# The order of a Winograd tail, the order of its loads, the queue of its stores, and the additional matmuls, in a hybrid decoder block

## The chip, the cores and the metric

The kernel runs on one core of a Trainium2 chip. The metric is the device time of one execution in microseconds; lower is better. Time before: 2496.36 us, the median of 3 runs (2493.04 to 2498.78).

## What is computed

One layer of a decoder trunk on 512 tokens of width 2048, all in float32:

```python
h = rmsnorm(x, g_mix)
z = h @ w_in                       # 2048 x 10248
cb, cc, cv, q, k, v, f_logit, gate_c, gate_a = split(z)
conv_y = cb * causal_dwconv(cc * cv, conv_w)            # three taps
conv_branch = conv_y @ w_conv_out
attn = forgetting_attention(q, k, v, log_sigmoid(f_logit + b_f))   # 8 heads of 128, causal
attn_branch = attn @ w_attn_out
merged = sigmoid(gate_c + b_c) * conv_branch + sigmoid(gate_a + b_a) * attn_branch
x = x + merged @ w_mix_out
h = rmsnorm(x, g_mlp)
u = square(relu(h @ w_ff1))        # 2048 x 8192
x = x + u @ w_ff2
out = rmsnorm(x, g_final)
```

## The kernel before

**Products.** Each float32 operand is split in two parts of TensorE's rounded float32 type: ScalarE writes the high part `hi` (line 100), VectorE the low part `lo` as the difference (line 101). A product is three matmuls: high times high, high times low, low times high.

**Groups.** The products with `w_in` and `w_ff1` are done by Strassen's method in Winograd's form, seven products of half size in place of eight. The weights of two column blocks are four tiles `x00`, `x10`, `x01`, `x11` (1 MB each, [128, 8, 256]; first index: even or odd row blocks of 128, second: column block). The seven products have the names A11, A12, S1, S2, S3, S4, A22, after the sum of quarters of the activations that each needs; these sums, split in high and low parts, are made once for a whole stage. A `Group` (class at line 168) is done in two pieces: `head` makes A11 and A12, `tail` the other five. One product is a `run` (line 189): split the weights' tile into a pair of buffers `th`, `tl` (two of each), then 48 matmuls of 256 columns (`mm_cols`, line 126; `mm_rows`, line 145, for v). All matmuls with the high part come first, 32 of them, then the 16 with the low part. The accumulators a, b, c, d are banks of PSUM; `snap` (line 197) copies one to a tile `o` on ScalarE (five such tiles), `plus` (line 207) adds one to such a tile on VectorE, and `put` stores the result or passes it on.

In the tail of before, the order is S4, S2, S3, S1, A22. S4 uses the loaded `x11` as it is; the four others need differences of tiles, made in place on VectorE (line 104; 2048 elements for each partition):

```python
self.run(c, "S4", X[1, 1], True)
sub(X[0, 0], X[0, 1], X[0, 0])
sub(X[0, 1], X[1, 1], X[0, 1])
sub(X[1, 1], X[1, 1], X[0, 0])
self.run(a, "S2", X[1, 1], False)
```

There are four slots for weights' tiles; `load` takes the slot that came free first, `done` gives one back.

**The stages, in order.** Norm and transposes of x; heads of one v group and four k/q groups (about 24 to 85 us of the profile); the sums of activations; the five tails (85 to 231 us); one more v group of 260 columns; then six groups for the convolution's inputs, with the eight attention heads before the first four of them (275 to 480 us) and the eight jobs of the convolution (line 566) after them; eight groups for the gates (to 880 us); the two branch products and the mix product (to 1235 us); the sixteen groups of the first feed-forward product (to 1858 us; the first two have their heads ahead of both tails); the second feed-forward product and the last norm. Intermediate results go through device memory: `v_d`, `kq_d`, `z_d`, `g_d`, `y_d`, `a_d` and, for the squared feed-forward sums, `s_d`.

**Queues.** Loads of weights are issued from SP's queue (line 183), and so are the stores to `v_d`, `kq_d`, `z_d`, `g_d`, `y_d`, `a_d`. GpSimd's queue has the stores to `s_d` and `x1_d`, the loads of the sums and of x's blocks, and GpSimd's own few operations, among them a memset of two columns of `u` in each convolution job (line 571). Each queue, and each engine, takes its instructions in order. What order that is, a planner decides: it walks the program and gives out instructions by its own estimate of when they are ready, so that an engine's order is not always that of the text. Waits are put in from the data that instructions read and write.

**Additional matmuls.** `apart` (line 581) returns a function that `mm_cols` calls ahead of the matmuls of each q in the high part of S4. In before it issues two matmuls with 256 columns, at q = 2 and q = 5, into a bank `spare` that nobody reads. They are in one of the convolution's groups, three of the gates' and four of the feed-forward's.

Of the kernel before, what the change touches and what calls it, by code (L numbers as in the profile page):

```python
# [15 lines left out]
P = 128  # L16
# [4 lines left out]
HS = S // 2  # L21
# [15 lines left out]
QSCALE = float(P) ** -0.5  # L37
# [8 lines left out]
def tile_hybrid_block(ctx: ExitStack, tc, x, g_mix, w_in, b_f, b_gate, conv_w, w_conv_out,  # L46
# [79 lines left out]
    def mm_cols(ps, Sx, hi, lo, first, extra=None):  # L126


        ps = ps[0].rearrange("p (j s) -> p j s", j=2)
        nq = hi.shape[1]  # L130
        for part in range(2):
            for q in range(nq):
                Sh, Sl = Sx(q)
                if extra and part == 0:
                    extra(q, Sh, hi[:, q, :])
                for j in range(2):
                    o, js = ps[:, j, :], slice(j * P, (j + 1) * P)
                    if part == 0:
                        nc.tensor.matmul(o, hi[:, q, js], Sh, start=first and q == 0 and j == 0, stop=False,  # L139
                                         skip_group_check=True)  # L140
                        nc.tensor.matmul(o, hi[:, q, js], Sl, start=False, stop=False, skip_group_check=True)  # L141
                    else:
                        nc.tensor.matmul(o, lo[:, q, js], Sh, start=False, stop=q == nq - 1, skip_group_check=True)  # L143
# [24 lines left out]
    class Group:  # L168
# [67 lines left out]
            self.put(0, 0, s1)  # L236

        def tail(self):
            if self.at:
                X = self.X  # L240
            else:
                X = {(i, 0): self.load(i, 0) for i in range(2)}
            X[0, 1], X[1, 1] = self.load(0, 1), self.load(1, 1)
            a = self.a
            c = self.acc("c")
            self.run(c, "S4", X[1, 1], True)
            sub(X[0, 0], X[0, 1], X[0, 0])
            sub(X[0, 1], X[1, 1], X[0, 1])
            sub(X[1, 1], X[1, 1], X[0, 0])
            self.run(a, "S2", X[1, 1], False)  # L250
            sub(X[1, 0], X[1, 0], X[1, 1])
            self.done(1, 1)
            s2 = self.snap(a)
            while later:
                later.pop(0)()
            d = self.acc("d")
            self.run(d, "S3", X[0, 1], True)
            self.done(0, 1)
            d1 = self.snap(d, self.scale)
            self.run(a, "S1", X[0, 0], False)  # L260
            self.done(0, 0)
            s4 = self.snap(a, self.scale)
            add(d1, d1, s4)
            self.put(1, 1, d1)
            self.plus(s4, c, self.scale)
            self.put(0, 1, s4)
            self.run(d, "A22", X[1, 0], False)
            self.done(1, 0)
            self.plus(s2, d)
            self.put(1, 0, s2)  # L270
# [162 lines left out]
    def store_v(c0, w):  # L433
        def put(i, j, v):
            c = c0 + j * w
            n = min(w, AW - c)
            nc.sync.dma_start(out=v_d[2 * i:2 * i + 2, :, c:c + n].rearrange("t p c -> p t c"), in_=v[:, :, :n])
            if n < w:
                add(fl[:, 2 * i:2 * i + 2, :], v[:, :, n:], bf.unsqueeze(1).to_broadcast([P, 2, NH]))
        return put  # L440

    def store_kq(hp):
        def put(i, j, v):
            nc.sync.dma_start(out=kq_d[j, 2 * hp:2 * hp + 2, :, i * HS:(i + 1) * HS].rearrange("b p c -> p b c"), in_=v)
        return put

    cV = COL_AV + AW // 2
# [1 line left out]
    gV0 = Group(w_in, COL_AV, COL_AV + VW, VW, Q1.moving, mm_rows, ((4,), (3,), (6,), (7,)), store_v(0, VW))  # L449

    def kq(hp, banks):
        return Group(w_in, COL_K + hp * HS, COL_Q + hp * HS, HS, Q1.moving, mm_cols, banks, store_kq(hp), QSCALE)

    def steady(n):
        return ((2 + n % 2,), (3 - n % 2,), (0,), (1,))
# [73 lines left out]
    def attend(h):  # L529
        kT, qT = at("kT"), at("qT")  # L530
        nc.sync.dma_start(out=kT, in_=kq_d[0, h])
        nc.sync.dma_start(out=qT, in_=kq_d[1, h])
        vv = at("vv", [P, NT, P])
        nc.sync.dma_start(out=vv, in_=v_d[:, :, h * P:(h + 1) * P].rearrange("t p c -> p t c"))
        o = bank(4, "o")
        for qi in range(NT):
            n = (qi + 1) * P
            qs = slice(qi * P, n)
            sc = bank(5 + 2 * (qi % 2), "sc")
            nc.tensor.matmul(sc[:, :n], qT[:, qs], kT[:, :n], start=True, stop=False)  # L540
# [12 lines left out]
            nc.vector.tensor_scalar(out=p[:, :n], in0=p[:, :n], scalar1=rs, scalar2=None, op0=ALU.mult)  # L553
            tp = bank(6, "tp")
            for ki in range(qi + 1):
                nc.tensor.transpose(tp[:, ki * P:(ki + 1) * P], p[:, ki * P:(ki + 1) * P], ident)
            pt = at("pt")
            nc.vector.tensor_copy(pt[:, :n], tp[:, :n])
            for ki in range(qi + 1):
                nc.tensor.matmul(o[:, qs], vv[:, ki, :], pt[:, ki * P:(ki + 1) * P], start=(ki == 0), stop=(ki == qi))  # L560
        ov = at("ov")
        nc.scalar.activation(out=ov, in_=o, func=AF.Copy)
        nc.sync.dma_start(out=a_d[h], in_=ov)


    def conv_job(f):
        cv, cc, cb = at("cv"), at("cc"), at("cb")
        for k, t in enumerate((cb, cc, cv)):
            nc.sync.dma_start(out=t, in_=z_d[k, f])
        u = at("u", [P, S + 2])  # L570
        nc.gpsimd.memset(u[:, 0:2], 0.0)
        nc.vector.tensor_tensor(out=u[:, 2:], in0=cv, in1=cc, op=ALU.mult)
        w = [cwT[:, i * CT + f:i * CT + f + 1] for i in range(3)]
        y = at("y")
        nc.vector.tensor_scalar(out=y, in0=u[:, 0:S], scalar1=w[0], scalar2=None, op0=ALU.mult)
        for i in (1, 2):
            nc.vector.scalar_tensor_tensor(out=y, in0=u[:, i:S + i], scalar=w[i], in1=y, op0=ALU.mult, op1=ALU.add)
        nc.vector.tensor_tensor(out=y, in0=cb, in1=y, op=ALU.mult)
        nc.sync.dma_start(out=y_d[f], in_=y)

    def apart(i):


        spare = bank(i, "spare")

        def extra(q, Sh, h):
            if q in (2, 5):
                nc.tensor.matmul(spare[:, :HS], Sh[:, :P], Sh if q == 2 else h, start=True, stop=True)
        return {"S4": extra}

    n = 0
    for g in (4, 2, 0, 5, 3, 1):
        def put_z(i, j, v, g=g):
            f = 4 * (g % 2) + 2 * j
            nc.sync.dma_start(out=z_d[g // 2, f:f + 2, :, i * HS:(i + 1) * HS].rearrange("b p c -> p b c"), in_=v)
# [10 lines left out]
    for f in range(0, KT, 2):  # L606
        def put_g(i, j, v, f=f):
            for b in range(2):
                k = j * KT + f + b
                nc.scalar.activation(out=v[:, b, :], in_=v[:, b, :], func=AF.Sigmoid, bias=bgT[:, k:k + 1])  # L610
            nc.sync.dma_start(out=g_d[j, f:f + 2, :, i * HS:(i + 1) * HS].rearrange("b p c -> p b c"), in_=v)
# [259 lines left out]

    def ff1(g, banks):
        return Group(w_ff1, g * S, g * S + HS, HS, Q2.moving, mm_cols, banks, put_u(g),
                     extra=apart(0) if g % 4 == 2 else {})

    ph.close()
    ph = ExitStack()
# [201 lines left out]
```

## Time and profile before

| | |
|---|---|
| median of 3 runs | 2496.36 us |
| the profiled execution's own time | 2499.57 us |
| its span, first to last instruction | 2497.8 us |
| mean granted clock of TensorE | 0.996 |
| VectorE busy | 1902.0 us (76%) |
| ScalarE busy | 1149.4 us (46%) |
| GpSimd busy | 112.5 us (5%) |
| transfers, mean | 186 GB/s |

The profile is of one execution. PE is TensorE, DVE VectorE, ACT ScalarE, POOL GpSimd, SP the engine that only issues transfers; a q behind an engine's name is its queue. Times are counted from the start of the span. In tables of stretches, each row has a start and an end, the length, then the busy time of PE, PEld (loading of weights into the array), DVE, ACT and POOL with the number of their instructions, the granted clock, the share of the DMA engines and GB/s. In lists of waits, a row names who waited for whom, the total in us, the number of times and the longest. In groups of instructions, a row has line, engine, operation, output and inputs by the program's names, shapes and count, then busy time in us and mean ns of one, then idle time before them and what ended it. In lists of transfers, the last number is the median time in us from issue to landing. A matmul's own duration overlaps that of the next; its cost is the distance from start to start.

### The profile page before, as it was taken

The numbers are of one execution on the slowest core, as the hardware profiler recorded it, in microseconds if no ns is written. First come the engines' busy times: TensorE is split into PE (matmuls) and PEld (weight loads), VectorE is DVE, ScalarE is ACT, GpSimd is POOL, SyncE is SP. The second block draws the span as 40 slices with busy tenths as digits, with TensorE's granted clock in tenths as the row PEclk, the third lists the DMA queues.
The fourth block names the chain that finished last, engine by engine and source line by source line (L and its number), as shares of the span: only waits on it lengthen the run. The fifth ranks groups of instructions, "written<-read, shape, count | busy, mean of one in ns | idle before, by whom it ended". The sixth has DMA issues, their size and how long they took to land.

```text
span 2497.8 us, 39035 instructions
## 1 busy us (share of the span) xinstructions
PE 2444.2 (98%) x16911; PEld 2255.4 (90%) x16911; DVE 1902.0 (76%) x1498; ACT 1149.4 (46%) x1136; POOL 112.5 (5%) x184
## 2 busy tenths in 40 slices
PE   8999999999999999999999999999999999999997
PEld 8999989999999988888889999999998888888875
DVE  7877677789677844525678898898887888878888
ACT  6433433434544532225555666666654333333334
POOL 0000000000000000000000000000011000000010
PEclk9999999999999999999999999999999999999999
DMA  7554444456544554335645646656587556665472
GB/s 245 161 176 154 153 134 146 143 179 210 159 123 142 172 179 152 124 126 202 214 159 193 239 172 213 228 181 224 206 299 281 171 207 236 213 227 176 170 259 101
DMA packets 289919, 465.06 MB, mean 186 GB/s; under 512 B 10236, under 2 KB 194644, under 8 KB 289620
## 3 DMA queue, kind: packets, MB, share of 16 engines
q1 hardware_dynamic: 260704, 330.40, 40.8%
q0 software_dynamic: 28176, 131.08, 14.0%
q8 instruction: 132, 2.16, 0.4%
q10 hardware_dynamic: 868, 1.10, 0.1%
q14 instruction: 39, 0.32, 0.0%
HBM read 370.26 MB, written 92.27 MB: 185 GB/s over the span
## 4 chain that ended last, share of the span: by engine, by line
PE 72%; DVE 4%; DMA 3%; issue 2%; ACT 1%; POOL 0%; SPq 0%; POOLq 0%; ACTq 0%; DVEq 0%
PE a L139 5%; PE a L141 5%; PE a L143 5%; PE a L156 4%; PE a L157 4%; PE a L159 4%; PE d L141 3%; PE d L139 3%; PE d L143 3%; PE pt L301 2%; PE pn L310 2%; PE pn L308 2%; PE pt L303 2%; PE pn L309 2%; PE pt L302 2%; PE d L159 2%
## 5 line engine op out<-in xcount | busy, mean ns | idle before, releaser
L101 DVE TENSOR_TENSOR tl<-x,th 128x2048 fp32r<-128x2048 f32 (+1 forms) x252 | 574.7, 2288 | 216.4 <-ACT th L100 199.8
L100 ACT ACTIVATE th<-x 128x2048 fp32r<-128x2048 f32 (+1 forms) x252 | 482.6, 1918 | 497.4 <-PE a L141 181.1
L104 DVE TENSOR_TENSOR x<-x,x 128x2048 f32<-128x2048 f32 (+1 forms) x144 | 329.2, 2286 | 14.4 <-DMA x<-in_w_in_dram 8.6
L100 ACT ACTIVATE th<-y 128x2048 fp32r<-128x2048 f32 x80 | 153.7, 1922 | 245.5 <-PE a L157 153.7
L156 PE MATMUL a<-th,us 128*128 128x512 f32 x512 | 200.8, 392 | 7.9 <-ACT junk L334 3.4
L101 DVE TENSOR_TENSOR tl<-raw,th 128x2048 fp32r<-128x2048 f32 x40 | 91.7, 2293 | 151.9 <-ACT th L100 151.3
L157 PE MATMUL a<-th,us 128*128 128x512 f32 x512 | 200.4, 391 | 0.0
L101 DVE TENSOR_TENSOR tl<-y,th 128x2048 fp32r<-128x2048 f32 x80 | 182.7, 2283 | 8.1 <-ACT th L100 8.1
L139 PE MATMUL a<-ST,th 128*128 128x256 f32 x768 | 178.7, 278 | 5.8 <-ACT th L100 5.8
L141 PE MATMUL a<-ST,th 128*128 128x256 f32 x768 | 178.3, 278 | 0.0
L100 ACT ACTIVATE th<-raw 128x2048 fp32r<-128x2048 f32 x40 | 76.7, 1918 | 175.4 <-PE pt L302 62.6
L139 PEld LDWEIGHTS a<-ST,th 128*128 128x128 f32 x768 | 145.3, 189 | 6.4 <-ACT th L100 6.4
L141 PEld LDWEIGHTS a<-ST,th 128*128 128x128 f32 x768 | 145.3, 189 | 0.0
L139 PE MATMUL a<-S,th 128*128 128x256 f32 x576 | 135.2, 279 | 5.0 <-ACT th L100 5.0
L159 PE MATMUL a<-tl,us 128*128 128x512 f32 x512 | 136.9, 389 | 0.0
L141 PE MATMUL a<-S,th 128*128 128x256 f32 x576 | 134.5, 278 | 0.0
L100 ACT ACTIVATE th<-t 128x2048 fp32r<-128x2048 f32 x32 | 61.4, 1919 | 135.2 <-DVE t L104 68.9
L156 PEld LDWEIGHTS a<-th,us 128*128 128x128 f32 x512 | 96.6, 189 | 29.3 <-issue 3.8
L139 PE MATMUL d<-ST,th 128*128 128x256 f32 x512 | 118.0, 276 | 0.0
L141 PE MATMUL d<-ST,th 128*128 128x256 f32 x512 | 118.0, 276 | 0.0
L157 PEld LDWEIGHTS a<-th,us 128*128 128x128 f32 x512 | 96.8, 189 | 20.0
L159 PEld LDWEIGHTS a<-tl,us 128*128 128x128 f32 x512 | 96.2, 188 | 20.1
(284 smaller groups left out, 6281.2 us busy)
## 6 DMA issues: line engine op xcount, KB each, us to landing
x<-in_w_in_dram SPq DMA_DIRECT2D x86, 1024.0 KB, 5.9
x<-in_w_ff_dram SPq DMA_DIRECT2D x66, 1024.0 KB, 7.8
y<-in_w_ff_dram SPq DMA_DIRECT2D x64, 1024.0 KB, 7.4
us<-s_d POOLq DMA_DIRECT2D x48, 1024.0 KB, 9.3
s_d<-rh POOLq DMA_DIRECT2D x32, 896.0 KB, 5.1
s_d<-r POOLq DMA_DIRECT2D x32, 896.0 KB, 5.4
raw<-in_w_mix_out_dram SPq DMA_DIRECT2D x24, 1024.0 KB, 5.1
g_d<-o SPq DMA_DIRECT2D x32, 256.0 KB, 2.2
```

What stands on the lines that cost most here:

```text
L100: nc.scalar.activation(out=hi, in_=src, func=AF.Copy)
L101: nc.vector.tensor_tensor(out=lo, in0=src, in1=hi.bitcast(F32), op=ALU.subtract)
L104: nc.vector.tensor_tensor(out=out, in0=a, in1=b, op=ALU.subtract)
L139: nc.tensor.matmul(o, hi[:, q, js], Sh, start=first and q == 0 and j == 0, stop=False, skip_group_check=True)
L141: nc.tensor.matmul(o, hi[:, q, js], Sl, start=False, stop=False, skip_group_check=True)
L143: nc.tensor.matmul(o, lo[:, q, js], Sh, start=False, stop=q == nq - 1, skip_group_check=True)
L156: nc.tensor.matmul(o, Sh, hi[:, q, :], start=begin and q == 0, stop=False, skip_group_check=True)
L157: nc.tensor.matmul(o, Sl, hi[:, q, :], start=False, stop=False, skip_group_check=True)
L159: nc.tensor.matmul(o, Sh, lo[:, q, :], start=False, stop=q == nq - 1, skip_group_check=True)
L301: nc.tensor.matmul(ps[j], hi[:, q, js], xh, start=k == 0, stop=False)
L302: nc.tensor.matmul(ps[j], hi[:, q, js], xl, start=False, stop=False)
L303: nc.tensor.matmul(ps[j], lo[:, q, js], xh, start=False, stop=k == kt - 1)
```

## The change

Four things, in `mm_cols`, `Group.tail`, the `put` functions and `apart`:

- The tail's order is S1, S3, S2, S4, A22. S1 and then S4 are summed in c; d1 = S3 + c's S1 + a (each scaled); the sum of S1 and S4 is copied out of c and a is added to it. There are four `plus` and `add` operations in a tail where there were three, and all four read PSUM.
- The weights' tiles that a tail loads are loaded in the order `x01`, `x00`, `x11`, `x10`, where it was `x00`, `x10`, `x01`, `x11`.
- The stores to `v_d`, `kq_d`, `z_d`, `g_d`, `a_d` and `y_d` are issued from GpSimd's queue.
- `apart` issues one matmul with 192 columns, at q = 4, with the operands of a regular one, where it issued two with 256. It is used in five feed-forward groups (2, 5, 8, 11, 14) where it was four (2, 6, 10, 14). A new form, "first", issues one with 192 columns into the accumulator itself ahead of the first regular matmul of S3, which then overwrites it; it is used in the four k/q groups and in the first two feed-forward groups.

```diff
@@ mm_cols
-                if extra and part == 0:
+                if extra == "first" and part == 0 and q == 0:
+                    nc.tensor.matmul(ps[:, 0, :192], hi[:, q, :P], Sh[:, :192], start=True, stop=False,
+                                     skip_group_check=True)
+                elif extra and extra != "first" and part == 0:
                     extra(q, Sh, hi[:, q, :])
@@ Group.tail
-            if self.at:
-                X = self.X
-            else:
-                X = {(i, 0): self.load(i, 0) for i in range(2)}
-            X[0, 1], X[1, 1] = self.load(0, 1), self.load(1, 1)
+            X = self.X if self.at else {}
+            for ij in ((0, 1), (0, 0), (1, 1), (1, 0)):
+                if ij not in self.at:
+                    X[ij] = self.load(*ij)
             a = self.a
+            sub(X[0, 0], X[0, 1], X[0, 0])
             c = self.acc("c")
-            self.run(c, "S4", X[1, 1], True)
-            sub(X[0, 0], X[0, 1], X[0, 0])
+            self.run(c, "S1", X[0, 0], True)
             sub(X[0, 1], X[1, 1], X[0, 1])
-            sub(X[1, 1], X[1, 1], X[0, 0])
-            self.run(a, "S2", X[1, 1], False)
-            sub(X[1, 0], X[1, 0], X[1, 1])
-            self.done(1, 1)
+            d = self.acc("d")
+            self.run(d, "S3", X[0, 1], True)
+            sub(X[0, 1], X[1, 1], X[0, 0])
+            self.done(0, 0)
+            d1 = self.snap(d, self.scale)
+            self.plus(d1, c, self.scale)
+            self.run(a, "S2", X[0, 1], False)
+            sub(X[1, 0], X[1, 0], X[0, 1])
+            self.done(0, 1)
             s2 = self.snap(a)
             while later:
                 later.pop(0)()
-            d = self.acc("d")
-            self.run(d, "S3", X[0, 1], True)
-            self.done(0, 1)
-            d1 = self.snap(d, self.scale)
-            self.run(a, "S1", X[0, 0], False)
-            self.done(0, 0)
-            s4 = self.snap(a, self.scale)
-            add(d1, d1, s4)
+            self.plus(d1, a, self.scale)
             self.put(1, 1, d1)
-            self.plus(s4, c, self.scale)
+            self.run(c, "S4", X[1, 1], False)
+            self.done(1, 1)
+            s4 = self.snap(c, self.scale)
+            self.plus(s4, a, self.scale)
             self.put(0, 1, s4)
             self.run(d, "A22", X[1, 0], False)
@@ store_v, store_kq, attend, conv_job, put_z, put_g: each
-            nc.sync.dma_start(out=g_d[...], in_=v)
+            nc.gpsimd.dma_start(out=g_d[...], in_=v)
@@ kq
-        return Group(..., store_kq(hp), QSCALE)
+        return Group(..., store_kq(hp), QSCALE, extra={"S3": "first"})
@@ apart
-            if q in (2, 5):
-                nc.tensor.matmul(spare[:, :HS], Sh[:, :P], Sh if q == 2 else h, start=True, stop=True)
+            if q == 4:
+                nc.tensor.matmul(spare[:, :192], h[:, :P], Sh[:, :192], start=True, stop=True)
@@ ff1
-                     extra=apart(0) if g % 4 == 2 else {})
+                     extra={"S3": "first"} if g < 2 else apart(0) if g % 3 == 2 else {})
```

More of the change, by code (lines that the diff above doesn't have):

```diff
@@ L436, in put @@
             n = min(w, AW - c)
-            nc.sync.dma_start(out=v_d[2 * i:2 * i + 2, :, c:c + n].rearrange("t p c -> p t c"), in_=v[:, :, :n])
+            nc.gpsimd.dma_start(out=v_d[2 * i:2 * i + 2, :, c:c + n].rearrange("t p c -> p t c"), in_=v[:, :, :n])
             if n < w:
@@ L443, in put @@
         def put(i, j, v):
-            nc.sync.dma_start(out=kq_d[j, 2 * hp:2 * hp + 2, :, i * HS:(i + 1) * HS].rearrange("b p c -> p b c"), in_=v)
+            nc.gpsimd.dma_start(out=kq_d[j, 2 * hp:2 * hp + 2, :, i * HS:(i + 1) * HS].rearrange("b p c -> p b c"), in_=v)
         return put
@@ L451, in kq @@
     def kq(hp, banks):
-        return Group(w_in, COL_K + hp * HS, COL_Q + hp * HS, HS, Q1.moving, mm_cols, banks, store_kq(hp), QSCALE)
+        return Group(w_in, COL_K + hp * HS, COL_Q + hp * HS, HS, Q1.moving, mm_cols, banks, store_kq(hp), QSCALE,
+                     extra={"S3": "first"})
     def steady(n):
@@ L562, in attend @@
         nc.scalar.activation(out=ov, in_=o, func=AF.Copy)
-        nc.sync.dma_start(out=a_d[h], in_=ov)
+        nc.gpsimd.dma_start(out=a_d[h], in_=ov)
     def conv_job(f):
@@ L578, in conv_job @@
         nc.vector.tensor_tensor(out=y, in0=cb, in1=y, op=ALU.mult)
-        nc.sync.dma_start(out=y_d[f], in_=y)
+        nc.gpsimd.dma_start(out=y_d[f], in_=y)
     def apart(i):
@@ L594, in put_z @@
             f = 4 * (g % 2) + 2 * j
-            nc.sync.dma_start(out=z_d[g // 2, f:f + 2, :, i * HS:(i + 1) * HS].rearrange("b p c -> p b c"), in_=v)
+            nc.gpsimd.dma_start(out=z_d[g // 2, f:f + 2, :, i * HS:(i + 1) * HS].rearrange("b p c -> p b c"), in_=v)
         if n < NH // 2:
@@ L610, in put_g @@
                 nc.scalar.activation(out=v[:, b, :], in_=v[:, b, :], func=AF.Sigmoid, bias=bgT[:, k:k + 1])
-            nc.sync.dma_start(out=g_d[j, f:f + 2, :, i * HS:(i + 1) * HS].rearrange("b p c -> p b c"), in_=v)
+            nc.gpsimd.dma_start(out=g_d[j, f:f + 2, :, i * HS:(i + 1) * HS].rearrange("b p c -> p b c"), in_=v)
         whole(Group(w_in, COL_GC + f * P, COL_GA + f * P, HS, Q1.moving, mm_cols, steady(n), put_g,
```

## Prediction

> **What bounds the kernel now.** I read the page's busy shares first, then the table of stretches, then TensorE's waits, then the order of time around one wait.
>
> ```profile
> PE 2444.2 (98%) x16911; PEld 2255.4 (90%) x16911; DVE 1902.0 (76%) x1498; ACT 1149.4 (46%) x1136; POOL 112.5 (5%) x184
> ```
>
> TensorE is busy for 98% of the span, so only two things can shorten it: the few places where it waits, and the distance from one matmul to the next. Both show in the table of stretches (length, then busy time and instruction count of each engine, then the granted clock).
>
> ```profile
> 85.00:231.00 146.00, 139.17 (x1206) 137.98 (x1205) 111.33 (x61) 56.97 (x41) 0.00 (x0) 1.00 0.55 170
> 480.00:625.00 145.00, 145.00 (x1269) 144.86 (x1268) 125.57 (x97) 61.40 (x52) 0.81 (x8) 1.00 0.61 194
> 625.00:741.00 116.00, 116.00 (x986) 116.00 (x986) 82.99 (x47) 57.79 (x59) 0.00 (x0) 1.00 0.45 137
> 741.00:880.00 139.00, 139.00 (x1228) 139.00 (x1226) 102.97 (x68) 74.77 (x82) 0.00 (x0) 1.00 0.50 162
> 1258.00:1341.00 83.00, 75.84 (x636) 75.05 (x635) 68.44 (x47) 44.62 (x44) 3.29 (x6) 0.98 0.50 169
> 1341.00:1858.00 517.00, 517.00 (x4561) 517.00 (x4560) 452.36 (x338) 326.21 (x328) 33.42 (x60) 1.00 0.61 215
> ```
>
> All six hold matmuls with 256 columns. The third and the fourth row are the same kind of work (groups of the gates, TensorE never idle), yet a matmul takes 116.00/986 = 117.6 ns in one and 139.00/1228 = 113.2 ns in the other. So there are two spacings, 4.4 ns apart, at the same clock. The last row, 517.00/4561 = 113.3 ns, is almost all short spacing. With 113.2 ns as the floor, what each stretch has above it is: 85 to 231, 146.0 - 1206 x 0.1132 = 9.5 us; 480 to 625, 1.35; 625 to 741, 4.4; 1258 to 1341, 11.0; 1341 to 1858, 0.7. These 27 us are what the change can reach; there the engines wait as follows.
>
> ```profile
> PE a L139 <- ACT th L100: 10.8, 7, 2.8
> PE c L139 <- ACT th L100: 1.4, 1, 1.4
> PE c L159 <- DVE tl L101: 1.1, 1, 1.1
> ```
>
> The seven waits of the first row are starts of S2, four of them in the k/q tails and three in the first feed-forward groups. One of them in order of time (start, duration, engine, line; in brackets the idle time before and its releaser):
>
> ```profile
> 142.20 2.29 DVE L104 TENSOR_TENSOR x<-x,x 128x2048 f32<-128x2048 f32 x1 [0.33 <-DMA x<-in_w_in_dram]
> 144.41 2.29 DVE L101 TENSOR_TENSOR tl<-x,th 128x2048 fp32r<-128x2048 f32 x1
> 146.61 0.68 DVE L107 TENSOR_TENSOR o<-d,o 128x512 f32<-128x512 f32 x1
> 147.21 4.60 DVE L104 TENSOR_TENSOR x<-x,x 128x2048 f32<-128x2048 f32 x2
> 149.60 3.73 ACT L100 ACTIVATE th<-x 128x2048 fp32r<-128x2048 f32 x2 [5.43 <-DVE x L104]
> 148.58 1.98 PE L143 MATMUL c<-S,tl 128*128 128x256 f32 x16
> 151.57 0.39 PE L139 MATMUL a<-S,th 128*128 128x256 f32 x1 [1.01 <-ACT th L100]
> ```
>
> X11 lands last, at 142.2. S4 (its second part, 148.58) can start from the raw tile, but S2, the next run, needs X11 - (X01 - X00), and VectorE makes that behind the difference for S3 (142.20), S4's low part (144.41) and a sum (146.61); then ScalarE rounds it; TensorE waits 1.01 us. The old tail asks for no difference before its first run and, in the order of its text, for three before its second.
>
> The clock costs too. In the feed-forward heads, behind a wait of 2.76 us:
>
> ```profile
> 1297.69 0.58 PE L139 MATMUL a<-ST,th 128*128 128x256 f32 x1 [2.76 <-ACT th L100]
> 1298.07 0.41 PE L141 MATMUL a<-ST,th 128*128 128x256 f32 x1
> 1298.28 0.41 PE L139 MATMUL a<-ST,th 128*128 128x256 f32 x1
> ```
>
> The matmuls behind it are 0.21 us apart, and that stretch has a granted clock of 0.98 x 83 us, that is 1.7 us lost, inside the 11.0.
>
> **Order of tails and of loads.** The new order needs one difference before S1, one before S3, one before S2, none before S4, one before A22, and the loads come in that order. A run is 48 matmuls, 48 x 0.1132 = 5.4 us. Its part of VectorE is one low part and at most one difference:
>
> ```profile
> L101 DVE TENSOR_TENSOR tl<-x,th 128x2048 fp32r<-128x2048 f32 x245 | 558.5, 2287 | 203.5 <-ACT th L100 186.9 <-PE d L143 6.8 <-PE c L143 6.1
> L104 DVE TENSOR_TENSOR x<-x,x 128x2048 f32<-128x2048 f32 x140 | 319.9, 2285 | 14.4 <-DMA x<-in_w_in_dram 8.6 <-DMA x<-in_w_ff_dram 5.1
> L107 DVE TENSOR_TENSOR o<-c,o 128x512 f32<-128x512 f32 x31 | 21.2, 684 | 0.1
> L100 ACT ACTIVATE th<-x 128x2048 fp32r<-128x2048 f32 x245 | 469.0, 1917 | 479.3 <-PE a L141 178.0 <-DVE x L104 158.8 <-PE d L141 83.0
> ```
>
> 2.29 + 2.29 + 0.68 = 5.3 us in the fullest run, 5 x 2.29 + 4 x 2.29 + 4 x 0.68 = 23.3 us in a tail of 27.2. The rounding of a run is made about one run ahead, so the difference for S2 (after S3's low part, about 5.0 us after S1's start) plus 1.9 us of ScalarE is ready at 6.9 us where S2 starts at 10.9: 4 us of slack where the old order is 1 us late. Slots come free one after the other too: X01's successor is loaded after S2's difference, X10's after A22's rounding, and the last is wanted only for the fifth run. So the waits of the k/q tails go; I leave 1.0 us for dips: **-8.5 us** (ends: 0, if the planner keeps VectorE as late as now, and -9.5).
>
> In 1258 to 1341 the same two waits go, and S1's operand is the first that the sums before it make. But VectorE has 68.4 us of work there, plus one further sum in each of three tails (below), 70.5 us, against a floor of 636 x 0.1132 = 72.0 for TensorE. In-order VectorE cannot run at 98% without a hole; in 1341 to 1858 it runs at 452.36/517.00 = 87% without making TensorE wait. I take half with the half clock: **-6.0 us** (ends 0 and -11.0).
>
> The tail has one more sum out of PSUM: two into d1 and one each into s4 and s2, where before one of three was in SBUF; 0.68 us of VectorE for each tail. Its cover is VectorE's idle 13% in 1341 to 1858 (64.6 us against about 14 x 0.68 = 9.5). Without that cover it would add up to those 9.5 us. Bank a is now read until after S4; the next group's first run takes b's bank, so nothing waits for that. At nothing.
>
> **Stores in GpSimd's queue.** The 8 stores of v, 16 of kq, 24 of z, 32 of g, 8 of a, 8 of y leave SP's in-order queue, where loads stood behind them, and go behind whatever GpSimd waits for:
>
> ```profile
> SPq L611 <- DVE o L107: 107.1, 29, 9.1
> POOL u L571 <- DVE y L577: 122.4, 7, 46.9
> L852 POOL DMA_DIRECT2D s_d<-rh x32 | 17.2, 538 | 535.2 <-ACT rh L849 483.5 <-ACT o L833 51.8
> g_d<-o SPq DMA_DIRECT2D x32, 256.0 KB, 2.2
> s_d<-rh POOLq DMA_DIRECT2D x32, 896.0 KB, 5.1
> ```
>
> A store now costs GpSimd about 0.54 us, and it is idle in these stretches. What a store can be late by is the wait of the memset of u, up to 46.9 us; who would wait for it is ScalarE's next copy into an o tile. There are five o tiles, four for each group of about 38 us, so a store has some 38 us before anyone waits. On the other side, no wait of TensorE above goes back to a load that stood behind a store. At nothing (ends 0, as there is no such wait to remove, and +9, for one store 46.9 us late).
>
> **The additional matmuls.** Before, sixteen (two in each of eight S4 runs); after, fifteen with 192 columns. What one does to the spacing is seen here, with `spare` as the output:
>
> ```profile
> 740.33 0.28 PE L141 MATMUL c<-S,th 128*128 128x256 f32 x1
> 740.45 0.28 PE L588 MATMUL spare<-th,S 128*128 128x256 f32 x1
> ...
> 741.16 0.28 PE L141 MATMUL c<-S,th 128*128 128x256 f32 x1
> 741.27 0.28 PE L139 MATMUL c<-S,th 128*128 128x256 f32 x1
> 741.39 0.28 PE L141 MATMUL c<-S,th 128*128 128x256 f32 x1
> 853.36 0.28 PE L141 MATMUL c<-S,th 128*128 128x256 f32 x1
> 853.47 0.28 PE L588 MATMUL spare<-S 128*128 128x256 f32 x1
> 853.59 0.28 PE L139 MATMUL c<-S,th 128*128 128x256 f32 x1
> ```
>
> The second of a pair (740.45) ends the long spacing: the stretch before it is the 117.6 ns row, the one behind it the 113.2 ns row. The first of a pair (853.47) starts it: 0.11 us before, 0.12 after. So an odd matmul can switch the spacing either way, by what it is and not by the spacing it finds. The new one has the regular operands and a quarter fewer columns; no row shows one. Nearest is the second of a pair, the one that follows regular matmuls and leaves the short spacing, and I take that value. Then 625 to 741 gains 4.4 us, or nothing if a dip after the last one starts the long spacing again: **-4.0 us**. In 480 to 625 the one in the first of these groups moves three runs later (S4 is now fourth), 144 x 4.4 ns = 0.6 us worse at most, against 1.35 to gain: 0. The matmuls themselves: 16 x 0.113 = 1.8 us before, 15 x 0.113 x 192/256 = 1.3 after, an estimate, and half of the 0.7 us in 1341 to 1858: **-0.9 us**.
>
> The attention stretch I leave as it is, ±2 us: its waits are those of the softmax chain. Sum: -8.5 - 6.0 - 4.0 - 0.9 = -19.4 us. The profiled execution took 2499.57 us (span 2497.8 and 1.8 around it), 3.2 above the median; 2499.57 - 19.4 = 2480.2, and against the median 2496.36 - 19.4 = 2477.0.
>
> **Rivals.** *The spacing stays as it falls.* The lone matmul switches nothing; the order alone counts: -8.5 - 6.0 - 0.5 = -15, 2481, and up to 2491 if the half in 1258 to 1341 and half of the k/q waits stay as well (-5). For it: no row shows a lone one. Against it: all four second ones end in short spacing. [...]
>
> *The lone matmul starts the long spacing (slower).* Then all that now runs short behind one turns long: 1206 - 288 in the k/q tails, about 600 in 480 to 625, 1228, and 4561, together 7300 x 4.4 ns = +32 us, against -14.5 from waits and -0.5: +17, 2513. It decides from 15/0.0044 = 3400 matmuls on. For it: the first of a pair does just this. Against: that one has its weights and its columns both from the sums' tile, the new one has not.
>
> *VectorE becomes the bound in feed-forward.* Its 452.36 us become 462 of 517, and in-order waits on PSUM lie differently; 1 us for each of 14 groups is +14, which leaves -5: 2491.
>
> *The change doesn't do what it says.* The planner already issues in another order than the text (the difference at 142.20 belongs to the tail that follows, the sum at 146.61 to the one before), and might undo the order: 2496.
>
> **How the numbers follow.** Forecast 0.58; spacing as it falls 0.18; VectorE the bound 0.08, of which 0.07 still faster; nothing 0.03; long spacing 0.13, slower. With the edges: faster by over 0.2% (5 us, about what a measurement of this kernel can tell) 0.82, within 0.04, slower 0.14. Low end: all bounds together, -9.5 - 11.0 - 4.4 - 1.35 - 1.5 - 2 = -30, 2466. High end: the weak cases of the faster rivals, 2492. Beyond it is the long spacing and no change.
>
> **What would show it.** TensorE's waits for L100 on a in the k/q tails gone from the list; 85 to 231 done in about 137.5 us; TensorE's clock in the feed-forward heads at 1.00; every stretch of 256-column matmuls at 113.2 ns; DVE near 89% in feed-forward with TensorE never idle. It is wrong if the stretches behind the lone matmuls stand at 117.6 ns, if new waits for th show inside steady groups, or if ScalarE waits for o tiles.

## The result: slower, and the profile after

The changed kernel takes 2552.75 us (median of 6 runs, 2549.09 to 2555.91), the kernel before 2494.91 beside it (6 runs): ratio 1.0227, 95% interval 1.0214 to 1.0239. The profiled execution has a span of 2550.6 us. The forecast was 2477, its range ended at 2492.

The page after, busy shares and the chain that ended last:

```profile
PE 2460.1 (96%) x16910; PEld 2265.1 (89%) x16910; DVE 1924.6 (75%) x1536; ACT 1148.5 (45%) x1136; POOL 178.5 (7%) x280
...
PE 50%; issue 20%; DVE 4%; DMA 4%; ACT 2%; POOL 1%; POOLq 0%; ACTq 0%; DVEq 0%; SPq 0%
PE a L159 4%; PE a L160 4%; PE a L162 4%; DMA s_d<-r 3%; PE pn L311 2%; PE pt L305 2%; PE pn L312 2%; PE pn L313 2%; PE pt L304 2%; PE pt L306 2%; PE d L162 2%; PE d L159 2%; PE d L160 2%; DVE tl L101 1%; PE c L142 1%
```

A store, `s_d<-r`, has 3% of the chain, and TensorE is busy for 96% where it was 98%. Where the time went shows in the lengths of the stages, from the first matmul of one to the first of the next, in each kernel's trace, and in the last row to the start of the last matmul (us; the last column is the kernel with the old tails in the first feed-forward product, below):

| stage | before | after | old tails in feed-forward |
|---|---|---|---|
| five tails on w_in, one v group | 190.6 | 181.7 | 181.7 |
| attention, first convolution groups | 204.7 | 203.2 | 203.4 |
| convolution and gates | 399.9 | 395.2 | 394.8 |
| branch and mix products | 354.5 | 354.5 | 354.5 |
| first feed-forward product | 625.9 | 692.2 | 630.4 |
| second feed-forward product | 623.5 | 623.8 | 621.0 |

All groups on w_in together won 15 us (forecast: 8.5 and 4.0, and 2 either way in attention); the sixteen groups of the first feed-forward product lost 66. The table of stretches, first before, then after, for the start of that product and for all of it:

```profile
1235.00:1311.00 76.00, 70.20 (x592) 69.38 (x591) 59.63 (x50) 41.74 (x47) 3.47 (x5) 0.98 0.49 160
1235.00:1861.00 626.00, 616.41 (x5396) 615.22 (x5394) 540.22 (x408) 386.51 (x392) 40.26 (x71) 1.00 0.59 208
```

```profile
86.00:223.50 137.50, 137.50 (x1204) 137.50 (x1203) 111.81 (x66) 55.27 (x41) 10.88 (x15) 1.00 0.60 181
...
1221.00:1297.00 76.00, 73.90 (x636) 73.20 (x634) 60.25 (x51) 40.08 (x45) 3.48 (x5) 1.00 0.51 163
1221.00:1913.00 692.00, 636.42 (x5394) 628.55 (x5393) 554.01 (x427) 388.36 (x392) 38.90 (x69) 0.98 0.55 192
```

Practically the same number of matmuls, 5394, takes 66 us longer. TensorE's idle time goes from 626.00 - 616.41 = 9.6 us to 692.00 - 636.42 = 55.6; its busy time is 20 us longer, and the granted clock, 0.98 over 692 us where it was 1.00, is some 14 of these, an estimate from the rounded clock. VectorE has 554.01 us of work in 692, 80%: it is not short of time. Who waits there (1300 to 1915, TensorE; and in another answer VectorE and ScalarE, 1200 to 1890):

```profile
PE a L142 <- ACT th L100: 17.4, 13, 2.2
PE b L146 <- DVE tl L101: 14.3, 8, 1.8
PE a L159 <- issue: 11.1, 1, 11.1
PE b L142 <- ACT th L100: 6.2, 4, 5.3
```

```profile
DVE r L107 <- ACT r L836: 96.1, 23, 7.4
...
ACT r L836 <- DMA s_d<-r: 66.0, 14, 5.8
...
ACT r L841 <- DMA s_d<-r: 22.1, 15, 7.3
```

So ScalarE waits 29 times for a landing before it fills `r`, 88.1 us in all. In before, in the same window, it does so twice:

```profile
ACT r L833 <- DMA s_d<-r: 4.0, 2, 3.9
```

The instruction for which VectorE has the long wait (96.1 us) is the first sum into `r`. As a group of 1341 to 1858, in before and in after (the number behind the bar is the idle time just ahead of it, which in before is nothing):

```profile
L107 DVE TENSOR_TENSOR r<-o,r 128x256 f32<-128x256 f32 x27 | 11.2, 415 | 0.0
```

```profile
L107 DVE TENSOR_TENSOR r<-o,r 128x256 f32<-128x256 f32 x24 | 10.2, 424 | 81.8 <-ACT r L836 81.8
```

What `r` is: behind each group, `put_u` makes the seven sums of squares that the second product needs, in two halves. `sums(0)` runs when `later`, a list of work put off, is emptied in the next tail, `sums(1)` when both `put(1, 1)` and `put(0, 1)` have been called. Each fills the same tile `r` (7 KB a partition, one buffer), rounds it into `rh`, subtracts `rh` from it, and stores both to `s_d`, 896 KB each. The next filling must wait until the store of `r` has landed.

One such place in order of time, after:

```profile
1453.20 0.63 ACT L841 ACTIVATE r<-c 128x512 f32<-128x512 f32 x1 [0.86 <-DMA s_d<-r]
1469.15 0.53 POOL L856 DMA_DIRECT2D s_d<-r  x1 [4.21 <-issue]
1469.38 0.68 DVE L107 TENSOR_TENSOR o<-a,o 128x512 f32<-128x512 f32 x1
1476.38 0.42 ACT L836 ACTIVATE r<-o 128x256 f32<-128x256 f32 x1 [5.11 <-DMA s_d<-r]
1476.71 1.90 ACT L100 ACTIVATE th<-x 128x2048 fp32r<-128x2048 f32 x1
1476.84 0.43 DVE L107 TENSOR_TENSOR r<-o,r 128x256 f32<-128x256 f32 x1 [6.77 <-ACT r L836]
1478.66 0.39 PE L142 MATMUL a<-ST,th 128*128 128x256 f32 x1 [0.75 <-ACT th L100]
```

and the same step of before:

```profile
1456.12 0.62 ACT L838 ACTIVATE r<-c 128x512 f32<-128x512 f32 x1
1465.13 0.53 POOL L853 DMA_DIRECT2D s_d<-r  x1 [2.06 <-DVE r L850]
1475.17 0.42 ACT L833 ACTIVATE r<-o 128x256 f32<-128x256 f32 x1
```

After, `sums(0)` holds `r` from 1453.20 until its store is issued at 1469.15, 16.0 us where it was 9.0, since four splits and differences of 2.3 us stand between its small operations on VectorE, where in before it was one. `sums(1)` is wanted at once (ScalarE is free for it 5.11 us before 1476.38); before, it came 10.0 us after the store. Now ScalarE stands 5.11 us for the landing, VectorE 6.77 us for ScalarE, and behind both, in order, are the rounding (1476.71) and the low part that TensorE's next run needs.

### The profile page after: what moved, and what is told of

Read it like the earlier page. It is cut to its first block, busy times and chain, and to the rows that moved or that the text cites. A ratio compares the mean times of both kernels' runs of the same rounds, so it can differ in the third digit from the quotient of the medians.

```text
span 2550.6 us, 39183 instructions
## 1 busy us (share of the span) xinstructions
PE 2460.1 (96%) x16910; PEld 2265.1 (89%) x16910; DVE 1924.6 (75%) x1536; ACT 1148.5 (45%) x1136; POOL 178.5 (7%) x280
## 4 chain that ended last, share of the span: by engine, by line
PE 50%; issue 20%; DVE 4%; DMA 4%; ACT 2%; POOL 1%; POOLq 0%; ACTq 0%; DVEq 0%; SPq 0%
PE a L159 4%; PE a L160 4%; PE a L162 4%; DMA s_d<-r 3%; PE pn L311 2%; PE pt L305 2%; PE pn L312 2%; PE pn L313 2%; PE pt L304 2%; PE pt L306 2%; PE d L162 2%; PE d L159 2%; PE d L160 2%; DVE tl L101 1%; PE c L142 1%
## 5 line engine op out<-in xcount | busy, mean ns | idle before, releaser
L100 ACT ACTIVATE th<-x 128x2048 fp32r<-128x2048 f32 (+1 forms) x252 | 481.3, 1915 | 400.5 <-DVE x L104 140.9
L100 ACT ACTIVATE th<-y 128x2048 fp32r<-128x2048 f32 x80 | 153.8, 1922 | 241.0 <-PE a L160 151.7
L100 ACT ACTIVATE th<-raw 128x2048 fp32r<-128x2048 f32 x40 | 76.8, 1920 | 176.3 <-PE pt L305 71.5
L142 PE MATMUL a<-ST,th 128*128 128x256 f32 x512 | 123.8, 285 | 19.1 <-ACT th L100 19.1
L142 PE MATMUL c<-S,th 128*128 128x256 f32 x576 | 134.7, 278 | 0.8 <-DVE o L107 0.8
L144 PE MATMUL c<-S,th 128*128 128x256 f32 x576 | 134.4, 278 | 0.0
L142 PE MATMUL c<-ST,th 128*128 128x256 f32 x512 | 121.0, 281 | 3.6 <-DVE o L107 3.4
L100 ACT ACTIVATE th<-t 128x2048 fp32r<-128x2048 f32 x32 | 61.4, 1920 | 135.6 <-DVE t L104 71.8
L144 PE MATMUL a<-ST,th 128*128 128x256 f32 x512 | 122.0, 282 | 0.0
L144 PE MATMUL c<-ST,th 128*128 128x256 f32 x512 | 119.6, 278 | 0.0
L142 PEld LDWEIGHTS a<-ST,th 128*128 128x128 f32 x512 | 98.5, 192 | 21.9 <-ACT th L100 21.9
L160 PEld LDWEIGHTS a<-th,us 128*128 128x128 f32 x512 | 97.2, 190 | 20.2
```

The costliest lines, as they stand in the source:

```text
L100: nc.scalar.activation(out=hi, in_=src, func=AF.Copy)
L160: nc.tensor.matmul(o, Sl, hi[:, q, :], start=False, stop=False, skip_group_check=True)
```

## The experiments

The theory (A): the new order lets the two fillings of `r` follow so that a landing is no longer covered, and the cycle of `r` gets longer than a group's matmuls. Times of before beside the experiments were 2498.1 to 2499.9 us, so the ratios count. Lengths of stages are measured as in the table above.

**The place of `sums(0)` in the text.** The loop that empties `later`, moved from behind S2's copy to behind S1's run, or behind S3's run:

```diff
             self.run(c, "S1", X[0, 0], True)
+            while later:
+                later.pop(0)()
...
             s2 = self.snap(a)
-            while later:
-                later.pop(0)()
```

> The changed kernel with one edit: the held-back feed-forward sums (sums(0) of the group before, and hold) are made after S1's run instead of after S2's, so that sums(0) and sums(1), which share the single tile r, are three runs apart instead of one. Theory A (the single tile r: sums(1) may write r only when the store of sums(0)'s r has landed, and VectorE stands in order behind it): the waits of ScalarE's squares for s_d<-r go from 55.7 us to under 10, VectorE's waits for ScalarE's r from 81.8 us to under 20, the feed-forward stage (first matmul on its sums to first matmul of the second product, 692 us in the changed kernel and 626 in the one before) returns to 620 to 630, total 2475 to 2485. Theory B (VectorE has become the bound through its fourth sum per tail): VectorE's work is the same, so 2540 to 2555. Theory C (the new order of runs itself starves TensorE, S1 and S3 waiting for their differences): 2540 to 2555 too.

> The changed kernel with the held-back sums made after S3's run: sums(0) and sums(1) are two runs apart, which is the distance in the kernel before. Theory A: nearly as good as three runs, since before had two and no wait of TensorE: 2475 to 2490. Theories B and C: 2540 to 2555.

2529.99 us (ratio 1.0118, interval 1.0095 to 1.0141) and 2530.65 (1.0114, 1.0088 to 1.0139), both with 668 to 671 us in the product. Neither number had been expected: a third of the product's 66 us goes, wherever of the two the loop is put. In the first (1341 to 1860) the waits have become fewer and not gone:

```profile
DVE r L107 <- ACT o L836: 55.0, 13, 4.7
...
ACT r L836 <- DMA s_d<-r: 35.3, 13, 3.2
```

And the reverse, the kernel before with the loop moved one run later, behind S3's:

> The kernel before with one edit: the held-back sums are made after S3's run instead of after S2's, so that sums(0) and sums(1) are one run apart, as in the changed kernel; order of tails, loads, stores and additional matmuls as before. Theory A: the feed-forward stage gets its waits here too, 626 us becomes 660 to 690, total 2530 to 2560. Theories B and C: nothing in their cause is touched, 2490 to 2500.

2498.29 us, ratio 1.0007 (0.9987 to 1.0026), 623.1 us in the product: theory A missed. The trace shows why: `r` is held for 9.0 us by `sums(0)` and filled again 10.0 us after its store, as in before, so the planner issued these operations where it had them already. In the old order one run more or less in the text changes nothing, and the theory in that form fell; what was left to test was the tile itself.

**`r` never waits for its landing.** After, with the second store of `sums(0)`, and then of both halves, sending `rh` once more, so that the low parts of these sums are left out (the diff is the second, both halves; the first has `r if j else h.bitcast(F32)`):

```diff
-            nc.gpsimd.dma_start(out=s_d[g // 2][:, 1, q], in_=r)
+            nc.gpsimd.dma_start(out=s_d[g // 2][:, 1, q], in_=h.bitcast(F32))
```

> The changed kernel, in which the second store of sums(0) sends the high part h once more instead of the low part r (the low part of these sums is left out, the number and size of transfers stay), so that nothing has to land before sums(1) may write r. Sums stay one run apart. Theory A in its strict form (it is the landing of r's store): ScalarE's waits for s_d<-r in its squares go to near 0, total 2480 to 2505. If it is the closeness of the two blocks of VectorE's and ScalarE's work itself, not the landing: 2520 to 2555. Theories B and C: 2540 to 2555.

> The kernel after, with the store of the low part replaced in both halves of a group: in the place of `r` it sends `rh` a second time, so the same bytes go over the same queue, but `r` never waits for a landing (left out: the low parts of these sums). Theory A (the single tile `r` is held until its store lands, and VectorE stands behind that): the earlier kernel that did this in one half of each group came out at 2489.6 us with 631 us in the first feed-forward product, and 22 us of waits for ScalarE's work on r were left; here these go too, so that product takes 622 to 627 us and the whole 2480 to 2486. Rival B (what was left, 631 against 625.9 before, comes from the new order itself, subtractions ahead of splits): product 629 to 633, whole 2488 to 2492. Rival C (`rh`, which is still stored from a single tile, takes over as the one that is waited for): product 640 or more, whole over 2498.

With one half 2489.6 us (0.9956, 0.9940 to 0.9973), 631.2 us in the product; with both 2483.93 (0.9936, 0.9916 to 0.9957), 623.3; both lie in theory A's ranges. The stretch and TensorE's waits (1298 to 1850) of the second:

```profile
1222.00:1845.00 623.00, 613.58 (x5393) 611.99 (x5392) 554.03 (x427) 388.25 (x392) 38.66 (x69) 1.00 0.61 211
```

```profile
PE a L159 <- issue: 4.3, 1, 4.3
PE a L142 <- ACT th L100: 2.9, 1, 2.9
```

Bytes, queue, instructions, order of the text and VectorE's 554 us are those of after; what is missing is the wait of `r` for its landing, twice a group, and with it the whole loss. The planner's own order moves with that wait, so it is not held fixed. Order of runs, added sums and additional matmuls cost nothing by themselves in this product.

**The same wait put into the kernel before.** Its store of `r` issued twice to the same place, one after the other:

```diff
             nc.gpsimd.dma_start(out=s_d[g // 2][:, 1, q], in_=r)
+            nc.gpsimd.dma_start(out=s_d[g // 2][:, 1, q], in_=r)
```

> The kernel before with the store of the low part sent twice to the same place, one after the other, so that `r` comes free one landing (4 to 5 us) later; the order of runs is that of before. In before a filling of `r` starts 6.2 us and 10.1 us after the two stores of a cycle have been issued, so some 2 and 6 us of cover are left beside a landing of 4.1 us. Theory A (the hold of `r` against the group's 38.1 us sets the loss): the cover at the 6.2 us place is gone, 2 us and more a group would show as waits of ScalarE for the landing of `r`, part of it taken up by the slack of the other half: 5 to 35 us longer, 2503 to 2533. Rival (the hold does not matter in the old order, only what the new order does to the splits): within 3 us of before, 2496 to 2502, without such waits.

2636.48 us, ratio 1.0544 (1.0525 to 1.0563), 752.6 us in the product: the direction right, and the size some four times the upper end, as the cover at both places was smaller than I had reckoned (in before the store of `r` takes 3.9 to 9.5 us to land, 6.8 in the median, not 4.1) and the half clock adds to it (granted 0.93). Its waits, 1341 to 2000:

```profile
ACT r L838 <- DMA s_d<-r: 143.7, 14, 12.5
DVE r L107 <- ACT r L833: 131.2, 15, 11.6
PE a L139 <- ACT th L100: 51.1, 9, 7.7
```

The old order fails in the same way once the landing is uncovered. This run adds more than a landing, though: 896 KB more of stores a half, and a wait in GpSimd's queue between the two stores (175.3 us in all). The cycle of `r` is read from the copies that begin `sums(0)`, each in 1400 to 1660; a row has line, engine, operation, count, durations in ns, first and last start (before; after; both halves without the landing; the store twice):

```profile
L838 ACT ACTIVATE r<-c x7: 610/614/620, 1418.0 to 1646.8; 128x512 f32<-128x512 f32 x7
```

```profile
L841 ACT ACTIVATE r<-c x6: 633/634/635, 1411.3 to 1623.8; 128x512 f32<-128x512 f32 x6
```

```profile
L841 ACT ACTIVATE r<-c x7: 617/626/635, 1430.2 to 1658.9; 128x512 f32<-128x512 f32 x7
```

```profile
L838 ACT ACTIVATE r<-c x6: 630/632/634, 1405.1 to 1638.1; 128x512 f32<-128x512 f32 x6
```

That is 228.8/6 = 38.1 us a group, 212.5/5 = 42.5, 228.7/6 = 38.1 and 233.0/5 = 46.6. TensorE has 336 matmuls a group, 336 x 113.3 ns = 38.1 us. Over the 14 steady groups 4.4 us more is 62 of the 66 us lost. TensorE's wait ahead of the second product, 11.1 us where before had 2.4, adds 9, and the first 76 us give back 5. The distance from copy to copy is the length of a group whatever sets it, so it says where the loss lies; that `r` sets it is read from the waits for its landing and from the runs without them.

**Operations on `r` ahead of others.** After, with the body of `sums` given out by the planner ahead of all other ready work:

> The kernel after, with the operations that fill `r`, split it and store it put ahead of all other ready work in the planner, so that on VectorE fewer splits and differences of 2.3 us stand between them. Theory A (the cycle of `r`: two fillings, two stores, each filling held up by VectorE's other work, 40 to 42 us where a group has 38.1 us of matmuls): a shorter hold brings the cycle under 38.1 us again; two of the differences between are about 5 us, so 2 to 4 us a group over 14 groups, 28 to 56 us less: 2497 to 2525. Rival G (only where the second filling starts counts, and this the order of runs sets, S4's copy and the last sum following within one run): the wait for the landing stays, 2540 to 2555. If the splits for TensorE come late because r's work is ahead of them, new waits for th and tl appear inside runs.

2528.66 us (1.0105, 1.0077 to 1.0133), 664.4 us in the product: just beyond the range of A and below that of G. The cycle is 40.6 us. `sums(0)` holds `r` for 11 to 13 us in place of 14 to 16, but the first square of `sums(1)` still comes 8 to 9 us after that store, and the next group's copy 4 to 6 us after the other; VectorE waits 57.4 us. So a shorter hold is worth some 28 us of the 66 (692.2 - 664.4); this order of the planner's does not cover the rest.

**The new tail on w_in only, and there with two groups more.** The sixteen tails of the first feed-forward product as in before (S4, S2, S3, S1, A22 and its loads), all else as after; then the first two of them new again. The diff is of the first, without the text of `tail_before`, which is the old tail; in the second, `heads` keeps `g.tail()`:

```diff
     for g in heads:
-        g.tail()
+        g.tail_before()
...
-        group.tail()
+        group.tail_before()
```

> The kernel after in all but one thing: the sixteen tails of the first feed-forward product are written in the order and with the loads of before (S4, S2, S3, S1, A22); all groups on w_in keep the new tail, and stores and additional matmuls are those of after. Theory A (the loss is the order's effect on the tile `r`, which exists only in this product): the product is back at 623 to 627 us, and the gain of 8.9 us in the tails and 4.7 us in convolution and gates stays, so 2480 to 2486 us. Rival D (the stores in GpSimd's queue or the additional matmuls carry part of the loss in that product, since both are as in after): product over 632 us, whole over 2490. Rival E (the gain ahead of it was lent, given back where the waits end): 2494 or more.

> As the kernel with the tails of before in the first feed-forward product, but its first two groups, which stand behind both heads, have the new tail, which has no earlier group's sums to make at its start. Theory A says that the new order costs where the two fillings of `r` of one group and of the next follow at a run's distance; two groups of sixteen would give back about 2/16 of the 66 us, 8 us, if they behaved like the others: 2488 to 2493. Rival F (the prediction's term: these two groups wait about 11 us in before for weights and copies in the stretch 1258 to 1341 and the new order takes 6 of them away): 2474 to 2480. In between (2481 to 2487): both or neither, undecided from the total, and then read from the waits of that stretch.

2489.26 us (0.9957, 0.9944 to 0.9970) and 2491.97 (0.9968, 0.9956 to 0.9980), with 630.4 and 633.4 us in the product. Both are faster than both kernels, the first by 10 us than before. It lies 3 us above theory A's range, and its product between A's range and rival D's: of the 66 us 62 are back, 4.5 are not. TensorE's waits for `th` there come to 11.4 us (before: 7.2), which is 4 of the 4.5; why they are more is not shown. The second lies in the range that theory A gave it, but the two intervals overlap, so that the difference between the two is read from one trace each. The stretches of the product's start in the first and in the second:

```profile
1222.00:1298.00 76.00, 70.74 (x591) 69.95 (x590) 59.58 (x49) 41.34 (x46) 3.48 (x5) 0.98 0.49 160
1298.00:1374.00 76.00, 72.35 (x634) 71.76 (x633) 64.73 (x49) 45.72 (x47) 4.26 (x8) 1.00 0.54 185
```

```profile
1225.00:1301.00 76.00, 73.89 (x628) 73.20 (x627) 59.91 (x50) 40.04 (x46) 3.48 (x5) 0.98 0.51 161
1301.00:1377.00 76.00, 68.31 (x578) 67.72 (x577) 63.46 (x47) 45.26 (x47) 4.25 (x8) 0.96 0.51 177
```

The new order gains where `r` is not yet in use: 628 matmuls against 591 in 76 us, 37 x 113.3 ns = 4.2 us. In the next 76 us, with the first sums, it loses 56 matmuls, 6.3 us.

**Additional matmuls and stores.** On the kernel with the old feed-forward tails: the matmuls of before, no additional matmul at all, and the stores back in SP's queue.

> The kernel that has the tails of before in the first feed-forward product and is otherwise as after (2489.3 us, gates part 394.8 us), now with the additional matmuls of before in place of the new ones: no lone matmul in the k/q tails and in the first two feed-forward groups, two of 256 columns in place of one of 192 in the gates, every fourth group in place of every third. Theory M (the prediction's term: the long spacing in the gates goes because of the new matmuls, 4.0 us): gates part back at 399 to 400, whole 2492 to 2496. Rival N (the spacing falls as it falls; kernels that are alike up to that point have shown 394.8, 395.2, 397.9 and 398.0 us there): anywhere in 394 to 400, and the whole within 3 us of 2489.

> As the one before it, but with no additional matmul anywhere (none in the k/q tails, the gates and the first feed-forward product). The matmuls themselves are worth under 1 us. Theory M: without any, the long spacing holds on wherever it has begun: over the 400 us of convolution and gates and the 626 us of the first feed-forward product it would cost up to 4.3 ns on each of some 8000 matmuls, 34 us, if it held throughout, and 4 us or more in any case: 2493 to 2520. Rival N: 2486 to 2492.

> The kernel that has the tails of before in the first feed-forward product and is otherwise as after (2489.3 us), with the stores of v, k/q, z, gates, convolution and attention back in SP's queue. The prediction's term: moving them is worth nothing (0 to 9 us either way): 2486 to 2492. Rival P (the gain of 8.9 us in the tails is the stores', which no longer stand ahead of the weights' loads on SP and wait for VectorE there): the tails back at 186 to 191 us and the whole at 2494 to 2499. If the order of loads carries the gain, the tails stay at 181 to 183.

2491.48 us (ratio 0.9966, 0.9951 to 0.9980), 2492.40 (0.9966, 0.9944 to 0.9988) and 2486.96 (0.9954, 0.9938 to 0.9969). The intervals overlap with that of the kernel they came from, so in the median none of the three is shown to matter. The trace tells more. With no additional matmul the long spacing held through the first feed-forward product in the profiled execution, 852 matmuls in 100 us where the kernel with them has 882 (the product took 644.4 us, with them 630.4):

```profile
1600.00:1700.00 100.00, 100.00 (x852) 100.00 (x851) 85.23 (x63) 60.42 (x59) 5.87 (x11) 1.00 0.62 211
```

```profile
1600.00:1700.00 100.00, 100.00 (x882) 100.00 (x883) 86.57 (x66) 64.71 (x65) 5.31 (x10) 1.00 0.63 219
```

This is 117.4 against 113.4 ns; that execution took 2505.39 us, others of the same kernel 2481.45 at the least: a scatter of 25 us, where the kernel with the new matmuls has 13.7, that with those of before 16.3, and that with the stores on SP, which has the new matmuls too, 20.2. Whether the additional matmuls narrow the scatter is therefore not shown. Theory M does not hold for the gates: convolution and gates took 396.7 us with the matmuls of before and 395.5 without any. In the tails on w_in the lone one shows: 87 to 270 without it and with it,

```profile
87.00:270.00 183.00, 183.00 (x1559) 183.00 (x1558) 143.18 (x91) 74.06 (x60) 14.54 (x20) 1.00 0.55 168
```

```profile
87.00:270.00 183.00, 183.00 (x1578) 182.28 (x1577) 145.44 (x94) 74.45 (x60) 14.51 (x20) 1.00 0.55 169
```

and the stage took 184.2 us in both kernels without it, 181.7 in all nine with it. With the stores on SP the stage stays at 181.7: the queue of the stores brings nothing.

## Why the prediction was wrong

**The step that failed** is the one that ends in "At nothing": the cost of the new tail in the first feed-forward product's steady groups. For the new order itself I had no term there. For the added sum I had set VectorE's added work (0.68 us a tail) against its idle 13%, and asked only whether a bank of PSUM is waited for. I did not ask when the tail's results reach `put_u`: there they fill a tile with one buffer whose store takes 4 us and more to land, and both engines that make TensorE's operands stand in order behind the one that waits. The rows were there to be read, `s_d<-rh` with 5.1 us to its landing beside a group of 38.1 us: two landings, two fillings, and 10.0 us between a store and the next filling that the new order shortens. The product measured +66 us, and without the waits for the landing nothing of it is left (623.3 us).

**Order and loads in the k/q tails, -8.5**: the stage is 8.9 us shorter, and 1204 matmuls are done in 137.5 us where it was 1206 in 146.0, about as said; the waits for L100 there are gone. But without the lone matmuls the stage takes 184.2 us, mostly at the long spacing (183.00/1559 = 117.4 ns). So 2.5 of the 8.9 hang on the lone matmuls, which I had left at nothing in that stretch, and the order and the loads alone have 6.4. That the number came out is in part luck.

**Feed-forward heads, -6.0**: 636 matmuls against 592 in the first 76 us, 44 x 113.3 ns = 5.0 us, with the clock at 1.00 as said. It was lost at once in the groups behind.

**Gates, -4.0**: not shown. The profile of after has 4.7 us less in convolution and gates, but by luck: the eight kernels that run the same instructions up to there (after, and the seven that change the first feed-forward product alone) took 394.8 to 398.0 us. Kernels with the matmuls of before took 394.6 to 399.9, those with the new ones 394.8 to 398.7. I had taken the one execution's long spacing for the kernel's; here the rival "the spacing stays as it falls" was right. The Trainium skill, "TensorE: Matmul & The Clock Gate", section "Back-to-back issue gap", gives 262 cycles for 256 columns as the gap of an isolated matmul, an estimate of 109 ns at the 2.4 GHz that it names there, and no second spacing. For a stream of weight loads and matmuls the Trainium skill says in the same section that both set the spacing, and has no figure for 256 columns. The traces, which are of such a stream, have 113.3 and 117.4 ns.

**The matmuls themselves, -0.9**: not shown; the kernel without any is not seen to be faster (2492.40 us, intervals overlapping).

**Stores, 0**: right (2486.96 us with them on SP, intervals overlapping).

**The rivals.** "The lone matmul starts the long spacing" did not happen; and that it switches nothing, as the rival right for the gates has it, does not hold in the k/q tails (181.7 us with it, 184.2 without). "VectorE becomes the bound" named the right stage and had 14 us by guess, for the wrong reason: VectorE is busy for 80%, and it waits. The prediction's own sign of being wrong, new waits for `th` inside steady groups, is what the profile shows.

**Open** is why the kernel with the old feed-forward tails waits more for `th` and needs 630.4 us there, not 625.9, and how much of the half clock behind the waits in after counts toward the 66 us (about 14 by the granted clock, an estimate). No run gave `r` a second buffer.

## What to carry to other kernels

When an order is changed, follow each result to the last buffer that it passes through, not only to the bank that it leaves: a tile with one buffer costs its filling, its work and the landing of its store, twice a group here, and that cycle must stay under the bound engine's. Look for what stands in order behind a wait; a pause of 5 us on ScalarE, with VectorE idle for a fifth of its time, moved TensorE. And a gain read from one profiled execution needs a second one before it is called the kernel's.

## What the runs showed of the hardware

Two steady spacings of the same matmul, 113.3 and 117.4 ns for 256 columns at a granted clock of 1.00, held for hundreds of microseconds, and chance had a part in which one. In the eight kernels that run the same instructions up to there, 3 to 773 of the 3476 distances in convolution and gates were long ones (115.6 to 125 ns). In the first feed-forward product 323 of 5386 matmuls stood less than 115.6 ns behind the one before in the kernel without additional ones, 4952 of 5394 in before. Short waits cost clock too: 4.4 us more in the cycle of `r` on 14 groups left TensorE 46 us idle and its clock at 0.98, and 8.5 us more, in the kernel with the store sent twice, at 0.93.
